# Pinned seven-product pairs with own raw buffers for the quarter chunk, and four gate pairs computed the same way

## The chip, the cores and the metric

The kernel runs on one core of one Trainium2 chip. The metric is the device time of one execution in microseconds. The engines are named as in the profile: PE is TensorE (matmuls), PEld its weight loads, DVE is VectorE, ACT is ScalarE, POOL is GpSimd, and SP is SyncE, which here issues DMAs only.

## The reference

One decoder layer on x of 512 tokens by 1024 channels, all in float32:

```python
proj = h @ w_in[l]
q, k, v, p, g = jnp.split(proj, ...)            # 512 each for q, k, v, p; 2048 gate logits
y_attn = moba_attention(q, k, v, rel_bias) @ w_branch_attn
y_pool = multiscale_pool(p, w_pool_group, pool_scale) @ w_branch_pool
gates = jax.nn.sigmoid(g).reshape(B, S, 2, D)
mixed = gates[:, :, 0] * y_attn + gates[:, :, 1] * y_pool
h = layer_norm(ALPHA * h + mixed @ w_out, ln1_g, ln1_b)
a, u = jnp.split(h @ w_ffn_in, 2, axis=-1)       # 2816 channels each
a = causal_dwconv(a, conv_w, conv_b)             # three taps
f = (jax.nn.gelu(a) * u) @ w_ffn_out
h = layer_norm(ALPHA * h + f, ln2_g, ln2_b)
```

Attention has 8 heads of 64 channels; the pool branch takes trailing means of 2, 4, 8 and 16 tokens.

## The kernel before

**Precision.** A float32 operand is split into a high part `hi` (a copy in the matmul's float32r type, on ACT, L69) and a low part `lo` (the rest, on DVE, L70). Each product of the mathematics is three matmuls, hi x hi, hi x lo and lo x hi (`mm3`, L183 to L186). Activations are kept transposed, channels on the partitions and 512 tokens along the free side.

**Weights.** The weights come as chunks of 128 x 1024 (512 KB), in one list `chunks` in order of use: v, the q/k/p/g tiles, the branch projections (`BR0`), the output projection (`WO0`), the FFN input (`FI0`) and the FFN output (`FO0`). `weights(i)` fetches up to `LEAD` = 3 chunks ahead of the one it returns, not past `state["limit"]`. `fetch` loads a chunk by SP into one of three raw buffers (tag `wraw`) and splits it into one of `RING` = 5 buffers each of `whi` and `wlo`.

**Stages.** v; then `in_tile` for the q, k, p and g tiles in the list `order`, 24 matmuls of 512 columns for a tile (8 blocks of the contraction, three matmuls each), with the g tiles as filler between the parts of the attention, pair of heads by pair of heads (`scores`, `trans`, `pv`; `bg` issues the next filler tile). There are 16 gate tiles, g0 to g15; tile f and tile 8 + f gate the same output channels of the two branches. The first twelve to be done are copied by DVE into `gates` (L355) and their sigmoid is taken later; the last four (`NLATE`) are written by ACT as sigmoids to `late`. After the attention, zT and oT (the outputs of the two branches before projection) are split, then the remaining gate tiles run, then the branch projection (`br`), the output projection (`wo`), layer norm, the FFN input (`fi`), the FFN output (`fo`), and the last layer norm.

**The seven-product pairs.** In the FFN input, f = 4 to 17 (`SEVEN`) take the pair of tiles (a, u), each 1024 x 128, as one block matrix with the tokens halved (t1, t2) and the contraction halved (k1, k2), and compute it with seven block products instead of eight, in Strassen's manner (`seven`, L693). The products use four combinations of the activations, nT1, T3, nT2 and T4 (`t_form`, L663, formed once), and four weight chunks for each f:

- A: the tile a, loaded by SP;
- X: u + a (with halves exchanged), loaded by SP as u (L131) and then added to by POOL with an accumulating DMA from a (L132); it goes to one of two buffers `xraw` (`fetch_sums`, called when X is within `AHEAD` = 5 chunks);
- D: half of u, 512 wide, loaded by SP into a `wraw` buffer;
- Y: formed by DVE from A and X in two halves (L144) in a `wraw` buffer.

A pair is seven groups (`s_mm`) of twelve matmuls of 256 columns, 84 in all, where two plain tiles have 48 of 512. The groups go to three banks, `sa`, `sb` and `sc`, in the order A, X, (the close of the pair before), Y, A, D, X. The close is the seventh group, on Y; DVE and ACT combine the products in between: the close needs DVE's addition of `y` and `sc` into `sa` (L711). Then comes `gated` (convolution, GELU, product).

**What sets the order.** The kernel is written in program order, and the framework schedules it: it simulates the engines by its own cost model and gives each engine a fixed queue, which the engine then runs in order, waiting at each instruction for its operands and for its output buffer. Only instructions issued under `tc.keep_in_program_order` keep their order among themselves.

Of the kernel before, what the change touches and what calls it, by code (L numbers as in the profile page):

```python
# [45 lines left out]
def layer_kernel(ctx: ExitStack, tc: tile.TileContext, xT, x, w_v, w_c, rel_bias, invcnt, w_group,  # L46
# [18 lines left out]
    def split(hi, lo, src, copy=None):  # L65
        if copy:
            copy(hi, src)
        else:
            nc.scalar.activation(hi, src, AF.Copy)  # L69
        nc.vector.tensor_tensor(lo, src, hi.bitcast(F32), op=ALU.subtract)  # L70

# [10 lines left out]
    chunks += [w_c[first[n] + j] for n, j in order]  # L82
    BR0 = len(chunks)
# [3 lines left out]
    FI0 = len(chunks)  # L87
    fi_at = {}
    for f in range(NF):
        for q in "AXDY" if f in SEVEN else "au":  # L90
            fi_at[f, q] = len(chunks)
            chunks.append((f, q) if f in SEVEN else w_fi[2 * f + "au".index(q)])
    FO0 = len(chunks)
# [28 lines left out]
    raws = {}  # L122
    sums = list(SEVEN)
    xu = None

    def fetch_sums(f):
        x_ = raws[f, "X"] = xu.tile([P, D], F32, tag="xraw", name=f"xraw{f}", bufs=2)
        a, u = w_fi[2 * f], w_fi[2 * f + 1]
        v = x_.rearrange("p (a c) -> p a c", a=2)
        (pst, pn), (est, _) = u.ap  # L130
        nc.sync.dma_start(v, bass.AP(tensor=u.tensor, offset=u.offset, ap=[[pst, pn], [0, 2], [est, S]]))  # L131
        nc.gpsimd.dma_start(v, bass.AP(tensor=a.tensor, offset=a.offset,  # L132
                                       ap=[[pst, pn], [u.offset + S - a.offset, 2], [est, S]]), accum_op=ALU.add)

    def fetch_seven(i, f, q):
        n = S if q == "D" else D
        if q == "X":
            raw = raws[f, "X"]
        else:
            raw = raws[f, q] = wp.tile([P, D], F32, tag="wraw", name=f"wraw{i}", bufs=3)[:, :n]  # L140
        if q == "Y":
            a, x_ = raws[f, "A"], raws[f, "X"]
            for c, o in ((slice(0, S), x_[:, S:]), (slice(S, D), raw[:, :S])):
                nc.vector.tensor_tensor(raw[:, c], o, a[:, c], op=ALU.add)  # L144
        elif q != "X":
            nc.sync.dma_start(raw, w_fi[2 * f] if q == "A" else w_fi[2 * f + 1][:, S:])
# [3 lines left out]
        return hi, lo  # L150

    def half(name, sl):
# [28 lines left out]

    def mm3(out_, w, a, start, stop, **kw):
        (wh, wl), (ah, al) = w, a  # L183
        nc.tensor.matmul(out_, wh, ah, start=start, stop=False, **kw)  # L184
        nc.tensor.matmul(out_, wh, al, start=False, stop=False, **kw)  # L185
        nc.tensor.matmul(out_, wl, ah, start=False, stop=stop, **kw)  # L186

# [153 lines left out]
    def in_tile(n):  # L341
        kind, j = order[n]
        wh, wl = split3(weights(C0 + n), KT)
        b = bank(f"{kind}{j}")
        for kt in range(KT):
            mm3(b, (wh[:, kt, :], wl[:, kt, :]), (xT_hi[:, kt, :], xT_lo[:, kt, :]), kt == 0, kt == KT - 1)
        if kind == "q":
            q_done(j, b)
        elif kind == "k":
            k_done(j, b)  # L350
        elif kind == "p":
            pool_in(j, b)
        elif len(gslot) < NKEEP:
            gslot[j] = gates[:, len(gslot), :]
            nc.vector.tensor_copy(gslot[j], b)  # L355
        else:
            gslot[j] = late[:, len(gslot) - NKEEP, :]
            nc.scalar.activation(gslot[j], b, AF.Sigmoid)

# [65 lines left out]
    def bg(n=1):  # L425
        for _ in range(n):
            if len(todo) > NLATE:
                t = todo.pop(0)
# [3 lines left out]
                if order[t][0] == "p":  # L432
                    due.append((t, order[t][1]))

    bg(3)
    for p in range(pairs):
        scores(2 * p)
        bg()
        scores(2 * p + 1)
        bg()  # L440
        trans(2 * p)
        bg()
        trans(2 * p + 1)
        bg()
        pv(p)
    bg(len(todo))
    attn.close()

    bra = ExitStack()
    bp = bra.enter_context(tc.tile_pool(name="bp", bufs=1, reuse_waits="tile"))  # L450
    late = bp.tile([P, NLATE, S], F32, name="late")
    zT_hi = bp.tile([P, 4, S], F32R, name="zT_hi")
# [5 lines left out]
    for k in range(4):  # L458
        split(oT_hi[:, k, :], oT_lo[:, k, :], oT[:, k, :])
    while todo:  # L460
        in_tile(todo.pop(0))
    mx_hi = act.tile([P, KT, S], F32R, tag="actT_hi", name="mx_hi")
    mx_lo = act.tile([P, KT, S], F32R, tag="actT_lo", name="mx_lo")
    ext = actp.enter_context(tc.tile_pool(name="ext", bufs=1, side="right"))
    for f in range(KT):
# [3 lines left out]
        for g in range(2):  # L469
            if gslot[8 * g + f].tensor is gates.tensor:  # L470
                nc.scalar.activation(gslot[8 * g + f], gslot[8 * g + f], AF.Sigmoid)
# [144 lines left out]
    def fi_mm(j, b, t):  # L616
        wh, wl = split3(weights(fi_at[j // 2, "au"[j % 2]]), KT)
        for kt in range(KT):
            mm3(b[:, t], (wh[:, kt, :], wl[:, kt, :]), (hT_hi[:, kt, t], hT_lo[:, kt, t]), kt == 0, kt == KT - 1)

# [29 lines left out]
    cuts = [slice(k, min(k + 4, KH)) for k in range(0, KH, 4)]  # L650
    t1, t2 = slice(0, 256), slice(256, 512)
    k1, k2 = slice(0, 4), slice(4, 8)

# [8 lines left out]

    def t_form(n):  # L663
        b11, b12, b21, b22 = (hraw[:, k, t] for k in (k1, k2) for t in (t1, t2))
        if n in ("nT1", "T3"):
            v, a = {"nT1": (b11, b11), "T3": (b12, b22)}[n]
            nc.vector.tensor_tensor(v, a, b12, op=ALU.subtract)
        else:
            v, a = {"nT2": (b22, b11), "T4": (b21, b22)}[n]
            nc.vector.scalar_tensor_tensor(v, a, -1.0, v, op0=ALU.mult, op1=ALU.subtract)  # L670
        split(*tt[n], v)

    for j in range(RING):
# [5 lines left out]
    for n in ("nT1", "T3", "nT2", "T4"):  # L679
        t_form(n)  # L680
    state["limit"] = len(chunks) - 1
    pending = []

    def s_mm(f, q, part, act_, b, start, skip=True):
        wh, wl = split3(weights(fi_at[f, q]), 4 if q == "D" else KT)
        for k in range(4):
            mm3(b, (wh[:, 4 * part + k, :], wl[:, 4 * part + k, :]), (act_[0][:, k, :], act_[1][:, k, :]),
                start and k == 0, k == 3, skip_group_check=not start)

    def whole(k, t):  # L690
        return hT_hi[:, k, t], hT_lo[:, k, t]

    def seven(f):  # L693
        ba, bb, bc = (bank(f"s{q}{f}") for q in "abc")
        chain, low, c11 = ba[:, 256:], bb[:, :256], bc[:, :256]
        y = ytiles[f % 2]
        u = xu.tile([P, S], F32, tag="u", name=f"u{f}", bufs=2)
        s_mm(f, "A", 0, whole(k1, t1), chain, True)
        nc.scalar.activation(y[:, t1], chain, AF.Copy)
        s_mm(f, "X", 0, tt["T3"], low, True)  # L700
        nc.scalar.activation(u[:, t2], low, AF.Copy)
        if pending:
            pending.pop()()
        s_mm(f, "Y", 0, tt["nT2"], chain, False)
        nc.scalar.activation(u[:, t1], chain, AF.Copy)
        s_mm(f, "A", 1, whole(k2, t1), c11, True)
        s_mm(f, "D", 0, tt["T4"], low, False)
        nc.vector.tensor_tensor(u[:, t1], u[:, t1], low, op=ALU.add)
        s_mm(f, "X", 1, tt["nT1"], chain, False)
        nc.vector.tensor_tensor(u[:, t2], u[:, t2], chain, op=ALU.add)  # L710
        nc.vector.tensor_tensor(ba[:, t1], y[:, t1], c11, op=ALU.add)  # L711

        def close():
            s_mm(f, "Y", 1, whole(k2, t2), chain, False)
            gated(f, ba, u, -1.0)

        pending.append(close)

    hr.close()
    xus = ExitStack()  # L720
    xu = xus.enter_context(tc.tile_pool(name="xu", bufs=1, reuse_waits="tile"))
    last = max(SEVEN)
    for f in range(RING // 2, last + 1):
        if f in SEVEN:
            seven(f)
            continue
        for j in range(max(RING, 2 * f), 2 * f + 2):
            hb[j] = bank(f"fi{j}")
            fi_mm(j, hb[j], slice(0, S))
            if pending:  # L730
                pending.pop()()
        gated(f, hb[2 * f], hb[2 * f + 1])

    spread = []
    for f in range(last + 1, NF):
        for j in range(2 * f, 2 * f + 2):
            hb[j] = bank(f"fi{j}")
            fi_mm(j, hb[j], slice(0, S))
            if pending:
                pending.pop()()  # L740
                xus.close()
# [191 lines left out]
```

## Time and profile before

| | |
|---|---|
| median of 3 runs | 651.3 us (651.03 to 653.6) |
| the profiled execution | 649.74 us, its span 648.0 us |
| granted TensorE clock, mean | 0.996 |
| busy PE, PEld | 635.7 us (98%), 551.4 us (85%) |
| busy DVE, ACT, POOL | 449.5 us (69%), 328.0 us (51%), 111.6 us (17%) |
| DMA | 94.79 MB, mean 146 GB/s |

In a row of the profile's timeline stand the start in us from the span's beginning, the duration, engine, line, operation, and the tiles written and read (numbers left out of names). `SPq` is a DMA issue on SP's queue. A bracket at the end tells how long the engine had stood idle and what ended it. In the windows, the columns after the stretch are its length, then busy us and instructions of PE, PEld, DVE, ACT and POOL, the granted TensorE clock, the DMA share and GB/s. A row of the waits reads: engine and tile that waited, the tile waited for, us in total, times, the longest. The rows of DMA issues give the number, the KB of each and the median us from issue to landing.

### The profile page before, as it was taken

The numbers are of one execution on the slowest core, as the hardware profiler recorded it, in microseconds if no ns is written. First come the engines' busy times: TensorE is split into PE (matmuls) and PEld (weight loads), VectorE is DVE, ScalarE is ACT, GpSimd is POOL, SyncE is SP. The second block draws the span as 40 slices with busy tenths as digits, with TensorE's granted clock in tenths as the row PEclk, the third lists the DMA queues.
The fourth block names the chain that finished last, engine by engine and source line by source line (L and its number), as shares of the span: only waits on it lengthen the run. The fifth ranks groups of instructions, "written<-read, shape, count | busy, mean of one in ns | idle before, by whom it ended". The sixth has DMA issues, their size and how long they took to land.

```text
span 648.0 us, 9322 instructions
## 1 busy us (share of the span) xinstructions
PE 635.7 (98%) x3586; PEld 551.4 (85%) x3586; DVE 449.5 (69%) x666; ACT 328.0 (51%) x475; POOL 111.6 (17%) x153
## 2 busy tenths in 40 slices
PE   9999999999999999999999999999999999999994
PEld 6888787877888888888999999998998888888884
DVE  6466665564532576299667888787986859698596
ACT  6547556675522333215444556455665337465452
POOL 1605361211000123300010101010100201123302
PEclk9999999999999999999999999999999999999998
DMA  9643222212222227404056686677635895989905
GB/s 323 197 166 99 82 81 82 74 67 89 74 95 98 91 98 286 136 1 162 2 150 173 170 208 155 179 179 188 165 128 163 274 264 137 218 188 193 282 4 129
DMA packets 32540, 94.79 MB, mean 146 GB/s; under 512 B 3688, under 2 KB 3944, under 8 KB 32240
## 3 DMA queue, kind: packets, MB, share of 16 engines
q1 hardware_dynamic: 22832, 66.91, 30.4%
q0 software_dynamic: 9088, 26.24, 20.7%
q10 hardware_dynamic: 576, 1.05, 0.5%
q8 instruction: 28, 0.46, 0.3%
q14 instruction: 16, 0.13, 0.1%
HBM read 91.02 MB, written 3.17 MB: 145 GB/s over the span
## 4 chain that ended last, share of the span: by engine, by line
PE 91%; DVE 3%; POOL 2%; DMA 1%; ACT 1%; issue 1%; DVEq 0%; ACTq 0%; POOLq 0%
PE fi L186 5%; PE fi L184 5%; PE fi L185 5%; PE g L184 5%; PE g L186 4%; PE g L185 4%; PE sa L184 4%; PE sa L186 4%; PE sa L185 4%; PE v L285 3%; PE wo L186 2%; PE br L186 2%; PE br L184 2%; PE wo L184 2%; PE wo L185 2%; PE br L185 2%
## 5 line engine op out<-in xcount | busy, mean ns | idle before, releaser
L70 DVE TENSOR_TENSOR wlo<-wraw,whi 128x1024 fp32r<-128x1024 f32 (+1 forms) x119 | 144.1, 1214 | 59.2 <-ACT whi L69 57.7
L69 ACT ACTIVATE whi<-wraw 128x1024 fp32r<-128x1024 f32 (+1 forms) x118 | 117.2, 996 | 131.9 <-PE g L185 23.6
L186 PE MATMUL fi<-hT_hi,wlo 128*128 128x512 f32 (+1 forms) x168 | 56.7, 339 | 0.0
L185 PE MATMUL fi<-hT_lo,whi 128*128 128x512 f32 (+1 forms) x168 | 56.7, 339 | 0.0
L184 PE MATMUL fi<-hT_hi,whi 128*128 128x512 f32 (+1 forms) x168 | 56.4, 340 | 0.0
L184 PE MATMUL g<-xT_hi,whi 128*128 128x512 f32 x128 | 50.3, 393 | 0.0
L186 PE MATMUL g<-xT_hi,wlo 128*128 128x512 f32 x128 | 49.9, 390 | 0.0
L185 PE MATMUL g<-xT_lo,whi 128*128 128x512 f32 x128 | 49.8, 389 | 0.0
L132 POOL DMA_DIRECT2D xraw<-in_w_fi x14 | 17.0, 1215 | 183.7 <-DVE y L624 70.2
L69 ACT ACTIVATE whi<-tw 128x1024 fp32r<-128x1024 f32 (+1 forms) x30 | 29.4, 982 | 21.6 <-DMA tw<-in_w_fo 8.1
L70 DVE TENSOR_TENSOR wlo<-tw,whi 128x1024 fp32r<-128x1024 f32 (+1 forms) x30 | 33.3, 1127 | 8.4 <-ACT whi L69 8.4
L185 PEld LDWEIGHTS fi<-hT_lo,whi 128*128 128x128 f32 x168 | 31.9, 190 | 3.5
L186 PEld LDWEIGHTS fi<-hT_hi,wlo 128*128 128x128 f32 x168 | 31.9, 190 | 3.3
L184 PEld LDWEIGHTS fi<-hT_hi,whi 128*128 128x128 f32 x168 | 31.6, 190 | 3.3
L184 PE MATMUL sa<-hT_hi,whi 128*128 128x256 f32 x112 | 31.9, 285 | 2.0 <-ACT whi L69 1.9
L186 PE MATMUL sa<-hT_hi,wlo 128*128 128x256 f32 x112 | 31.7, 284 | 0.0
L185 PE MATMUL sa<-hT_lo,whi 128*128 128x256 f32 x112 | 31.6, 283 | 0.0
L184 PE MATMUL sb<-T_hi,whi 128*128 128x256 f32 x112 | 31.5, 282 | 0.0
L184 PE MATMUL sa<-nT_hi,whi 128*128 128x256 f32 x112 | 31.5, 281 | 0.0
L186 PE MATMUL sa<-nT_hi,wlo 128*128 128x256 f32 x112 | 31.3, 279 | 0.0
L185 PE MATMUL sa<-nT_lo,whi 128*128 128x256 f32 x112 | 31.3, 279 | 0.0
L185 PE MATMUL sb<-T_lo,whi 128*128 128x256 f32 x112 | 31.3, 279 | 0.0
(250 smaller groups left out, 1762.8 us busy)
## 6 DMA issues: line engine op xcount, KB each, us to landing
wraw<-in_w_fi SPq DMA_DIRECT2D x30, 512.0 KB, 3.6
wraw<-in_w_c SPq DMA_DIRECT2D x28, 512.0 KB, 3.4
tw<-in_w_fo POOLq DMA_DIRECT2D x20, 512.0 KB, 8.3
xraw<-in_w_fi SPq DMA_DIRECT2D x14, 512.0 KB, 4.9
xraw<-in_w_fi POOLq DMA_DIRECT2D x14, 512.0 KB, 5.7
wraw<-in_w_fo SPq DMA_DIRECT2D x10, 512.0 KB, 5.1
tw<-in_w_fo SPq DMA_DIRECT2D x10, 512.0 KB, 6.6
wraw<-in_w_br SPq DMA_DIRECT2D x8, 512.0 KB, 3.3
```

Of the source, the lines that this page charges most:

```text
L69: nc.scalar.activation(hi, src, AF.Copy)
L70: nc.vector.tensor_tensor(lo, src, hi.bitcast(F32), op=ALU.subtract)
L132: nc.gpsimd.dma_start(v, bass.AP(tensor=a.tensor, offset=a.offset, ap=[[pst, pn], [u.offset + S - a.offset, 2], [est, S]]), accum_op=ALU.add)
L184: nc.tensor.matmul(out_, wh, ah, start=start, stop=False, **kw)
L185: nc.tensor.matmul(out_, wh, al, start=False, stop=False, **kw)
L186: nc.tensor.matmul(out_, wl, ah, start=False, stop=stop, **kw)
L285: nc.tensor.matmul(bs[j], xs_[j][a], (wh, wl)[b], start=kt == 0 and n == 0, stop=False)
```

## The change

Four things are changed.

1. All matmuls of the seven-product pairs are issued with `tc.keep_in_program_order`, and so are the matmuls of plain tiles while a close is pending (`pin` in `mm3`).
2. The chunk D gets raw buffers of its own: `draw`, two of them, in place of one of the three `wraw`.
3. The gate tiles g4 to g7 and g12 to g15 become four seven-product pairs. The list `order` now ends g2, g10, g3, then s4 to s7, then g11. For them x^T is fetched again in four quarters (`quad`, 512 KB each) and nT1, T3, nT2 and T4 of it are formed and split. The buffers (T-forms, two of `xrawg`, two of `drawg`, the quarters) lie in a pool `gx` in the space that the attention leaves. The sum X of a gate pair is fetched as in the FFN. `gates_done` takes both sigmoids on ACT straight from the result. All after T3's split is issued behind it (`issue_after`).
4. `late` moves to the other side of the memory, zT's and oT's splits come after the gate tiles, no gate pair's chunk is fetched until the attention is over (`state["limit"]`), and one filler tile at the last pair of heads is dropped.

`seven`, `s_mm`, `t_form` and the closing (`flush`) become general over the two uses. The core of the diff:

```diff
-    order += spare
+    order += [("g", 2), ("g", 10), ("g", 3)] + [("s", f) for f in range(4, KT)] + [("g", 11)]
...
+    for n, j in order:
+        at[n, j] = len(chunks)
+        if n == "s":
+            pair_of["g", j] = w_c[first["g"] + j], w_c[first["g"] + KT + j]
+            for q in "AXDY":
+                at["g", j, q] = len(chunks)
+                chunks.append((("g", j), q))
...
-        while sums and xu and fi_at[sums[0], "X"] <= i + AHEAD:
+        while sums and sums[0][0] in xpool and at[(*sums[0], "X")] <= i + AHEAD:
             fetch_sums(sums.pop(0))
...
-            raw = raws[f, "X"]
-        else:
-            raw = raws[f, q] = wp.tile([P, D], F32, tag="wraw", name=f"wraw{i}", bufs=3)[:, :n]
+            raw = raws[key, "X"]
+        elif q == "D":
+            raw = dpool[key[0]](key[1])
+        else:
+            raw = raws[key, q] = wp.tile([P, D], F32, tag="wraw", name=f"wraw{i}", bufs=3)
...
+    def t_form(n, tt, b11, b12, b21, b22):
...
+        if n != "nT1":
+            split_of[n] = split(*tt[n], v)
+        if n == "T4":
+            split(*tt["nT1"], b11)
...
+                start and k == 0, k == 3, tc.keep_in_program_order, skip_group_check=not start)
...
+        pin(nc.tensor.matmul(out_, wh, ah, start=start, stop=False, **kw))
+        pin(nc.tensor.matmul(out_, wh, al, start=False, stop=False, **kw))
+        pin(nc.tensor.matmul(out_, wl, ah, start=False, stop=stop, **kw))
...
+        if kind == "s":
+            seven(("g", j), (xT_hi, xT_lo), tg, p1s[j % 2], gus[j % 2],
+                  lambda ba, u, j=j: gates_done(j, ba, u))
+            return
...
+    def gates_done(j, ba, u):
+        nc.scalar.activation(new_gate(j), ba, AF.Sigmoid)
+        nc.scalar.activation(new_gate(KT + j), u, AF.Sigmoid, scale=-1.0)
...
+    gd = [gx.tile([P, S], F32, name=f"drawg{c}") for c in range(2)]
+    gr = [gx.tile([P, D], F32, name=f"xrawg{c}") for c in range(2)]
...
+            nc.sync.dma_start(v, xT[k.start * P:k.stop * P, t].rearrange("(k p) t -> p k t", p=P))
...
+    for n in ("nT1", "T3", "nT2", "T4"):
+        t_form(n, tg, *quads)
+    with ExitStack() as behind:
+        for ins in split_of["T3"]:
+            behind.enter_context(tc.issue_after(ins.ins))
+        while todo:
+            in_tile(todo.pop(0))
+        flush()
...
+    dpool["f"] = lambda f: xu.tile([P, S], F32, tag="draw", name=f"draw{f}", bufs=2)
+    xpool["f"] = lambda f: xu.tile([P, D], F32, tag="xraw", name=f"xraw{f}", bufs=2)
```

More of the change, by code (lines that the diff above doesn't have):

```diff
@@ L81, in layer_kernel @@
     C0 = len(chunks)
-    chunks += [w_c[first[n] + j] for n, j in order]
+    at = {}
+    pair_of = {}
+    for n, j in order:
[6 more added lines that the diff above has]
+        else:
+            chunks.append(w_c[first[n] + j])
     BR0 = len(chunks)
@@ L122, in layer_kernel, with fetch_sums @@
     raws = {}
[L123 to L128, printed above, removed]
+    sums = list(pair_of)
+    xpool = {}
+    dpool = {}
+    def fetch_sums(key):
+        x_ = raws[key, "X"] = xpool[key[0]](key[1])
+        a, u = pair_of[key]
         v = x_.rearrange("p (a c) -> p a c", a=2)
@@ L145, in fetch_seven @@
         elif q != "X":
-            nc.sync.dma_start(raw, w_fi[2 * f] if q == "A" else w_fi[2 * f + 1][:, S:])
+            a, u = pair_of[key]
+            nc.sync.dma_start(raw, a if q == "A" else u[:, S:])
         hi = wp.tile([P, D], F32R, tag="whi", name=f"whi{i}", bufs=RING)[:, :n]
@@ L426, in bg @@
         for _ in range(n):
-            if len(todo) > NLATE:
+            if order[todo[0]][0] != "s":
                 t = todo.pop(0)
@@ L469, in layer_kernel @@
         for g in range(2):
-            if gslot[8 * g + f].tensor is gates.tensor:
+            if 8 * g + f in plain:
                 nc.scalar.activation(gslot[8 * g + f], gslot[8 * g + f], AF.Sigmoid)
@@ L679, in layer_kernel @@
     for n in ("nT1", "T3", "nT2", "T4"):
-        t_form(n)
+        t_form(n, tt, *(hraw[:, k, t] for k in (k1, k2) for t in (t1, t2)))
     state["limit"] = len(chunks) - 1
[L682 to L717, printed above, removed]
     hr.close()
@@ L724, in layer_kernel @@
         if f in SEVEN:
-            seven(f)
+            seven(("f", f), (hT_hi, hT_lo), tt, ytiles[f % 2][:, t1],
+                  xu.tile([P, S], F32, tag="u", name=f"u{f}", bufs=2),
+                  lambda ba, u, f=f: gated(f, ba, u, -1.0))
             continue
```

125 lines of the change are left out of this document (87 added, 38 removed).

## The prediction

> **What bounds the kernel now.** I read the page first: which engine is full, and what ended the last wait on it.
>
> ```profile
> PE 635.7 (98%) x3586; PEld 551.4 (85%) x3586; DVE 449.5 (69%) x666; ACT 328.0 (51%) x475; POOL 111.6 (17%) x153
> PE   9999999999999999999999999999999999999994
> PE 91%; DVE 3%; POOL 2%; DMA 1%; ACT 1%; issue 1%; DVEq 0%; ACTq 0%; POOLq 0%
> xraw<-in_w_fi SPq DMA_DIRECT2D x14, 512.0 KB, 4.9
> xraw<-in_w_fi POOLq DMA_DIRECT2D x14, 512.0 KB, 5.7
> ```
>
> TensorE is busy in every slice and makes 91% of the chain that ended last, so fewer matmul columns shorten the kernel, as long as TensorE stays fed. The last two rows are the two transfers, one after the other, that make the chunk X = u + a of a pair; they decide my forecast. Next the stages that the change touches, by windows and by the timeline of PE:
>
> ```profile
> 180.00:212.00 32.00, 32.00 (x143) 26.50 (x142) 9.27 (x9) 9.01 (x12) 0.00 (x0) 1.00 0.29 99
> 367.00:389.00 22.00, 22.00 (x188) 22.00 (x187) 18.27 (x26) 12.42 (x19) 2.41 (x2) 1.00 0.73 191
> 399.00:412.00 13.00, 12.15 (x101) 11.80 (x100) 11.16 (x16) 8.10 (x12) 2.41 (x2) 1.00 0.60 169
> 434.00:445.00 11.00, 9.81 (x79) 9.38 (x79) 8.30 (x13) 5.18 (x7) 1.20 (x1) 1.00 0.74 174
> ```
>
> ```profile
> 179.87 0.39 PE L185 MATMUL g<-xT_lo,whi 128*128 128x512 f32 x1
> 180.09 0.39 PE L186 MATMUL g<-xT_hi,wlo 128*128 128x512 f32 x1
> ...
> 212.28 0.39 PE L184 MATMUL br<-zT_hi,whi 128*128 128x512 f32 x1
> ...
> 347.95 0.28 PE L184 MATMUL sa<-hT_hi,whi 128*128 128x256 f32 x1
> ...
> 410.84 0.28 PE L186 MATMUL sb<-T_hi,wlo 128*128 128x256 f32 x1
> 411.97 0.39 PE L184 MATMUL sa<-hT_hi,whi 128*128 128x256 f32 x1 [0.85 <-ACT whi L69]
> ...
> 441.98 0.28 PE L186 MATMUL sc<-hT_hi,wlo 128*128 128x256 f32 x1
> 443.34 0.39 PE L184 MATMUL sa<-hT_hi,whi 128*128 128x256 f32 x1 [1.08 <-ACT whi L69]
> ```
>
> The first window, gate tiles, is one unbroken row of 512-column matmuls, 32.00 / 143 = 0.224, by single starts 0.22 to 0.23 us; a tile of 24 takes 5.44. Gates end where br starts, 212.28. The seven-product stage begins at 347.95. Its 256-column matmuls are 0.117 us apart (22.00 / 188), TensorE's weight loading is then as full as TensorE, and a pair of 84 takes 9.97 at 0.1187, the mean over the stage. The last two windows are its only real holes: 411.97 - 410.84 and 443.34 - 441.98, less a pitch of 0.12 each, make 2.25, and the first matmul behind each takes 0.39 in place of 0.28: 2.5 us together.
>
> **The change part by part.** *Gate pairs.* Eight tiles of 24 (43.5 us) become four pairs of 84 (4 x 9.97 = 39.9): -3.7 if fed. *Pinning and own buffers for the quarter D.* Both holes are ACT splits of an A chunk that came late because its raw buffer, shared with D, came free late. With own buffers they go: -2.5. So the intent is worth -6.2.
>
> *What feeds TensorE.* Here the engines' orders decide, and each engine takes its queue in order. The present order around one X chunk, on DVE, SP and POOL:
>
> ```profile
> 403.58 0.68 DVE L144 TENSOR_TENSOR wraw<-xraw,wraw 128x512 f32<-128x512 f32 x1
> 404.19 1.22 DVE L70 TENSOR_TENSOR wlo<-xraw,whi 128x1024 fp32r<-128x1024 f32 x1
> 405.32 0.68 DVE L70 TENSOR_TENSOR wlo<-wraw,whi 128x512 fp32r<-128x512 f32 x1
> ...
> 406.52 0.74 DVE L624 SCALAR_TENSOR_TENSOR y<-sa,cvp,y 128x511 f32<-128x511 f32 x1
> ...
> 405.43 0.38 SPq L131 DMA_DIRECT2D xraw<-in_w_fi  x1
> ...
> 410.09 1.20 POOL L132 DMA_DIRECT2D xraw<-in_w_fi  x1 [8.22 <-DMA xraw<-in_w_fi]
> ```
>
> At 403.58 DVE forms the first half of Y(f), the sum of xraw(f) and A(f), and at 404.19 the low part of X(f) from the same xraw(f). That ends at 405.41; the buffer is free, and 0.02 us later SP loads u of pair f+2 into it; 4.66 us after that POOL adds a. So X(f+2) has two pairs' time, some 20 us, to come in, and the waits agree: by the row quoted below, DVE waited for an xraw transfer once in the whole run, at the start of the stage.
>
> In the changed program's order I find DVE forming Y(f+1) *ahead* of the low part of X(f), for f = 5 to 16. Y(f+1) needs xraw(f+1) complete; xraw(f+1) has the buffer of xraw(f-1) and is loaded only when DVE has done the low part of X(f-1). So a loop closes with one turn per pair: low part of X(f-1), SP's load, POOL's accumulation, Y(f+1) in two halves with a convolution step between, low part of X(f). Its turn, from the rows above and these (the landings of SP's loads, then of POOL's accumulations, the waits of DVE for xraw, and the low part of X(4)):
>
> ```profile
> DMA to landing us min/median/max: 3.6/4.9/6.5
> DMA to landing us min/median/max: 5.4/5.7/7.2
> ...
> 341.61 1.23 DVE L70 TENSOR_TENSOR wlo<-xraw,whi 128x1024 fp32r<-128x1024 f32 x1 [0.40 <-ACT whi L69]
> ...
> DVE wraw L144 <- DMA xraw<-in_w_fi: 4.9, 1, 4.9
> ```
>
> Load until POOL's issue: 5.2 (the median 4.9 with POOL's reaction; the row pair above gave 4.66). Accumulation 5.7. DVE 0.61 + 0.67 + 0.61 + 1.22 = 3.1 (start to start, the last to its end), handovers 0.1. Turn: 14.1 us, where TensorE needs a pair each 9.97. TensorE's third matmul on X(f) reads the low part, so it stands about 4 us per pair. The low part of X(4) ends at 342.8 (341.61 + 1.23) in the present timeline, whose stages before are the same work. Twelve turns lead to X(16): 342.8 + 12 x 14.1 = 512.0. Fed, TensorE would be there at 347.95 + 12 x 9.97 + 1.42 (the twelve matmuls of A) + 0.24 = 469.2. Late by 42.8; the closing group of pair 15 then waits for a DVE addition queued behind that low part, the splits of D and Y (0.7 and 1.2) and two other additions of some 0.4: 2.9 us, of which the rest of X's group covers 1, so about 2 more. X(17) is no longer in the loop, its buffer came free a turn earlier. Less the 2.5 of holes: +42.3. Bounds: at the shortest landings the turn is 3.6 + 5.4 + 3.2 = 12.2, +19.5; at 5.5 and 6.5 it is 15.2, +55.5; at both maxima 16.9, +76. I take the medians, as the same transfers run beside each other here (DMA share 0.60 to 0.74 in the windows).
>
> *Start of the gate pairs.* Around the end of attention:
>
> ```profile
> 141.95 0.40 PE L376 MATMUL sc<-kl,q 128*128 128x512 f32 x1
> ...
> 155.55 0.39 PE L185 MATMUL g<-xT_lo,whi 128*128 128x512 f32 x1
> ...
> 160.88 0.65 PE L417 MATMUL ob<-PT,vv 128*64 128x512 f32 x2
> ...
> 163.31 0.60 ACT L419 ACTIVATE oT<-ob 128x512 f32<-128x512 f32 x1 [0.96 <-PE ob L417]
> ...
> L667 DVE TENSOR_TENSOR hraw<-hraw x2: 1226/1226/1226, 316.1 to 317.4; 128x1024 f32<-128x1024 f32 x2
> ...
> 160.99 0.69 DVE L355 COPY gates<-g 128x512 f32<-128x512 f32 x1 [3.53 <-PE g L186]
> ```
>
> Both orders are the same up to 155.48. Then the changed TensorE queue has 17 matmuls of g3 (3.9 us) ahead of the end of the last ob (2.3 us): ob ends at 161.65. ACT copies oT, and the split of nT1 is queued behind that copy: 162.2 to 163.25. DVE waits for it and then has, in order: nT1's low part, T3, nT2, T3's low part (1.14 each start to start), the copy of g3 (0.61), T4, nT2's low part (1.14 each), half of Y(4) (0.61), and only then the low part of X(4) (1.22): 163.27 + 6 x 1.14 + 0.61 + 0.61 + 1.22 = 172.6. TensorE, with its remaining g3 and the group of A, would be at that operand at about 164.9: 7.7 us late. The loads hide: four fetches of x^T wait for the last score matmul and can go from 142.4 (141.95 + 0.40), and X(4) and X(5) behind them; their price without that cover would be one landing more, 5 us. The same loop then holds X(5) and X(6) (Y(6) stands ahead of X(5), Y(7) ahead of X(6)), without the convolution step: turn 13.4. X(6) has its low part at 172.6 + 2 x 13.4 = 199.4. Then the late close (+2.9), twelve groups of 1.424, g11 (5.44) and the last close (1.42): br starts at 226.3, that is +14.0 against 212.28, the -3.7 included. Bounds: turns of 11.5 give +10.2, of 14.5 give +16.2.
>
> The splits of zT and oT move behind the gates; four of each on ACT, by g11 and the close (6.9 us) covered, and uncovered they would cost some 4.5. The dropped filler tile and the direct sigmoids change where work lies and no amount: 0 (uncovered, a 0.6 ACT operation each).
>
> **Sum:** +42.3 + 14.0 = +56.3 on the profiled 649.74 is 706.0. The median of 651.3 is 1.6 above that execution: 707 against the median.
>
> [...] The accumulation took 5.4 at the least and 5.7 in the median. [...]
>
> **The rivals.** (1) *The sums are in time* and the plan holds: -6.2, 645. It needs a turn of at most 9.97, so both transfers in 6.8 us, where the shortest ones seen make 9.0; and the T-forms ready before 165, against ACT's order. For it: the present kernel streams the same bytes without a hole. It decides for faster as soon as the turn is under 9.97. Chance 0.06. (2) *The loop hides, the gate start does not*: +7.7 - 3.7 - 2.5 = +1.5, 653; the same condition on the turn, but the DVE queue at 163 stays. 0.04. (3) *Shorter transfers*: once TensorE stands 4 us per pair, other transfers thin out, and the accumulation has the queues alone. [...] Against it: the shortest accumulation of 14. 0.05. (4) *Longer turns* than 15.2, since X's load now goes out together with D's and A's each time: 723 and more, 747 at both maxima. 0.07.
>
> **How the numbers follow.** The forecast, a turn of 12.2 to 15.2, holds 0.78: 681 to 723 by its bounds (19.5 + 10.2 and 55.5 + 16.2 on the median), with 707 at the medians of the landings. The range 672 to 723 takes in (3) and leaves out (1), (2) and (4), 0.17. About 0.5% is what a measurement of this kernel can tell from no change: (1) is faster, 0.06; (2) within, 0.04; the rest slower, 0.90.
>
> **What would show it.** In the changed profile: in the seven-product stage X's low parts come some 14 us apart, TensorE's mean busy share there falls to about 0.7, its waits name wlo on DVE at the third matmul of sb, and next the addition sa on DVE; DVE's waits name the xraw transfers at the first half of Y, a dozen times. SP's X load starts right after a low part of X. Gates: the first sb of a gate pair waits till about 172, br starts near 226. I am wrong if br starts before 212, if the stage's pairs are 10 us apart, or if the two transfers together fall under 7 us.

## The result and the profile after

| | before | after |
|---|---|---|
| median of 4 runs, us | 651.22 (651.03 to 653.6) | 712.71 (711.69 to 713.98) |
| ratio, 95% interval | | 1.0936 [1.0903, 1.0969] |
| profiled execution: time, span | 649.74, 648.0 | 711.91, 710.2 |
| granted TensorE clock, mean | 0.996 | 0.962 |
| gates: last 128x512 copy of P^T on DVE to the first `br` matmul | 57.0 | 73.6 (+16.6) |
| FFN input: first matmul of a pair to the first `foe` matmul | 186.5 | 232.0 (+45.4) |

The kernel became slower by 9.4%. The two stages that the change touches hold all of it: 16.6 + 45.4 = 62.0, the spans differ by 62.2. From the page of after, the rows that answer to those of before, with the granted clock in 40 slices:

```profile
PE 656.8 (92%) x3730; PEld 574.7 (81%) x3730; DVE 468.3 (66%) x697; ACT 343.1 (48%) x499; POOL 114.2 (16%) x157
...
PE   8999999995889999999997987788779999999995
...
PEclk9999999998899999999999898889899999999999
...
xraw<-in_w_fi SPq DMA_DIRECT2D x14, 512.0 KB, 4.2
xraw<-in_w_fi POOLq DMA_DIRECT2D x14, 512.0 KB, 6.0
```

TensorE is full except in two places: slices 10 to 12, the start of the gate pairs, and slices 22 to 30, the seven-product pairs of the FFN. Its own busy time rose by 21 us, although the gate pairs have fewer columns: each matmul got longer where the clock fell (22.45 / 149 = 0.151 us of busy time at 0.82 in the second window below, 22.00 / 188 = 0.117 at 1.00 before). Windows of after (the columns as in the table of before):

```profile
364.71:398.00 33.29, 28.85 (x219) 28.45 (x218) 18.58 (x25) 14.18 (x23) 3.38 (x3) 0.90 0.57 138
454.00:482.00 28.00, 22.45 (x149) 21.63 (x149) 16.62 (x24) 11.40 (x17) 2.41 (x2) 0.82 0.53 132
528.20:542.00 13.80, 11.22 (x82) 11.02 (x81) 9.32 (x15) 5.50 (x10) 0.00 (x0) 0.88 0.24 77
```

Before, 22 us of this stage held 188 matmuls at a clock of 1.00; here 28 us hold 149 at 0.82. What TensorE and then DVE waited for, in the whole of after:

```profile
PE saf L253 <- DVE saf L213: 19.9, 11, 3.0
PE sbf L255 <- DVE wlo L70: 10.2, 5, 2.7
PE sbg L255 <- DVE wlo L70: 5.5, 3, 2.2
PE sbg L253 <- ACT whi L69: 5.4, 1, 5.4
```

```profile
DVE wraw L158 <- DMA xraw<-in_w_fi: 18.2, 5, 4.5
DVE wraw L158 <- issue: 14.5, 7, 2.7
```

DVE stood twelve times (5 + 7) at the first half of Y in the FFN, for 32.7 us; before, it stood there for an X transfer once. ("issue" is a wait for which the profile names no releaser. The turn below has one of these: the accumulation into its `xraw` landed at 398.55, and Y starts at 398.63.) TensorE's waits name the addition `saf` and the low part `wlo`, both of them DVE work queued behind that wait. The addition, on which the close waits, holds TensorE up for longer than the low part does (19.9 us against 10.2). One turn, by the timelines of DVE, SP, POOL and PE of after:

```profile
386.35 1.22 DVE L70 TENSOR_TENSOR wlo<-xraw,whi 128x1024 fp32r<-128x1024 f32 x1
387.59 0.38 SPq L143 DMA_DIRECT2D xraw<-in_w_fi  x1
392.42 1.21 POOL L144 DMA_DIRECT2D xraw<-in_w_fi  x1 [13.61 <-DMA xraw<-in_w_fi]
398.63 0.69 DVE L158 TENSOR_TENSOR wraw<-xraw,wraw 128x512 f32<-128x512 f32 x1 [1.94 <-issue]
399.24 0.74 DVE L738 SCALAR_TENSOR_TENSOR y<-saf,cvp,y 128x510 f32<-128x510 f32 x1
399.90 0.68 DVE L158 TENSOR_TENSOR wraw<-wraw,wraw 128x512 f32<-128x512 f32 x1
400.50 1.22 DVE L70 TENSOR_TENSOR wlo<-xraw,whi 128x1024 fp32r<-128x1024 f32 x1
...
387.62 0.38 PE L255 MATMUL sbf<-T_hi,wlo 128*128 128x256 f32 x1 [2.54 <-DVE wlo L70]
390.49 0.41 DVE L213 TENSOR_TENSOR saf<-y,scf 128x256 f32<-128x256 f32 x1
390.96 0.58 PE L253 MATMUL saf<-hT_hi,whi 128*128 128x256 f32 x1 [1.90 <-DVE saf L213]
```

The low part of X ends at 387.57, 0.02 later SP reloads the buffer, 4.83 later POOL adds, 6.21 later DVE can form Y, and 3.09 later the next low part has ended, at 401.72. Turn: 14.15. The chain of work that ended last can be followed back in after to about 519 us, and there it lies in the same loop (start, duration, piece):

```profile
519.47 3.85 DMA xraw<-in_w_fi
523.32 1.81 issue
525.13 0.69 DVE wraw L158
527.08 1.14 DVE wlo L70
```

At the gates:

```profile
163.04 0.60 ACT L503 ACTIVATE oT<-ob 128x512 f32<-128x512 f32 x1 [6.87 <-PE ob L501]
...
172.77 1.22 DVE L70 TENSOR_TENSOR wlo<-xrawg,whi 128x1024 fp32r<-128x1024 f32 x1
...
171.64 0.58 PE L253 MATMUL sbg<-gT_hi,whi 128*128 128x256 f32 x1 [5.39 <-ACT whi L69]
174.03 0.58 PE L255 MATMUL sbg<-gT_hi,wlo 128*128 128x256 f32 x1 [1.60 <-DVE wlo L70]
...
201.71 0.39 PE L255 MATMUL sbg<-gT_hi,wlo 128*128 128x256 f32 x1 [2.24 <-DVE wlo L70]
...
229.01 0.40 PE L253 MATMUL br<-zT_hi,whi 128*128 128x512 f32 x1
```

TensorE stood 7.0 us at the first X group of the gates, for ACT's split of X and then for DVE's low part of it, and 1.6 and 2.2 us at the X groups of the next two pairs.

### The profile page after: what moved, and what is told of

Read it like the earlier page. It is cut to its first block, busy times and chain, and to the rows that moved or that the text cites. A ratio compares the mean times of both kernels' runs of the same rounds, so it can differ in the third digit from the quotient of the medians.

```text
span 710.2 us, 9698 instructions
## 1 busy us (share of the span) xinstructions
PE 656.8 (92%) x3730; PEld 574.7 (81%) x3730; DVE 468.3 (66%) x697; ACT 343.1 (48%) x499; POOL 114.2 (16%) x157
## 5 line engine op out<-in xcount | busy, mean ns | idle before, releaser
L253 PE MATMUL saf<-hT_hi,whi 128*128 128x256 f32 x112 | 36.4, 325 | 19.9 <-DVE saf L213 19.9
L253 PEld LDWEIGHTS saf<-hT_hi,whi 128*128 128x128 f32 x112 | 24.4, 218 | 22.5 <-DVE saf L213 22.2
L255 PE MATMUL sbf<-T_hi,wlo 128*128 128x256 f32 x112 | 32.5, 290 | 10.3 <-DVE wlo L70 10.2
L255 PE MATMUL saf<-hT_hi,wlo 128*128 128x256 f32 x112 | 35.1, 313 | 0.0
L254 PE MATMUL saf<-hT_lo,whi 128*128 128x256 f32 x112 | 34.9, 311 | 0.0
L253 PE MATMUL saf<-nT_hi,whi 128*128 128x256 f32 x112 | 34.1, 304 | 0.0
L254 PE MATMUL saf<-nT_lo,whi 128*128 128x256 f32 x112 | 33.8, 301 | 0.0
L255 PE MATMUL saf<-nT_hi,wlo 128*128 128x256 f32 x112 | 33.6, 300 | 0.0
L253 PE MATMUL sbf<-T_hi,whi 128*128 128x256 f32 x112 | 31.8, 284 | 0.0
L254 PE MATMUL sbf<-T_lo,whi 128*128 128x256 f32 x112 | 31.6, 283 | 0.0
L158 DVE TENSOR_TENSOR wraw<-xraw,wraw 128x512 f32<-128x512 f32 x14 | 9.7, 692 | 33.1 <-DMA xraw<-in_w_fi 18.2
## 6 DMA issues: line engine op xcount, KB each, us to landing
wraw<-in_w_fi SPq DMA_DIRECT2D x30, 512.0 KB, 4.1
wraw<-in_w_c SPq DMA_DIRECT2D x24, 512.0 KB, 3.4
tw<-in_w_fo POOLq DMA_DIRECT2D x20, 512.0 KB, 8.2
xraw<-in_w_fi SPq DMA_DIRECT2D x14, 512.0 KB, 4.2
xraw<-in_w_fi POOLq DMA_DIRECT2D x14, 512.0 KB, 6.0
wraw<-in_w_fo SPq DMA_DIRECT2D x10, 512.0 KB, 5.8
tw<-in_w_fo SPq DMA_DIRECT2D x10, 512.0 KB, 6.7
wraw<-in_w_br SPq DMA_DIRECT2D x8, 512.0 KB, 3.6
```

What stands on the lines that cost most here:

```text
L253: pin(nc.tensor.matmul(out_, wh, ah, start=start, stop=False, **kw))
L254: pin(nc.tensor.matmul(out_, wh, al, start=False, stop=False, **kw))
L255: pin(nc.tensor.matmul(out_, wl, ah, start=False, stop=stop, **kw))
```

## The experiments

The theory to be tested: a scheduling order closes a loop (low part of X(f-1), reload, accumulation, Y(f+1), low part of X(f)), and the gate pairs start behind a long DVE queue. Against it stood: pinning TensorE costs time by itself; the transfers are slow by themselves; the lower clock, and not the wait, is the cause. All runs follow, each ratio against the kernel before as it ran beside them (its medians were 650.5 to 651.2). The two stages are measured as in the table above (change against before), in the profiled execution alone; the last copy of P^T stands at 155.3 to 157.5 us from one of them to the next, so the stages are compared and not the spans.

| run | median us | ratio [95%] | gates | FFN input | clock |
|---|---|---|---|---|---|
| after | 712.71 | 1.0936 [1.0903, 1.0969] | +16.6 | +45.4 | 0.962 |
| e5_pin_and_quarter | 694.1 | 1.0669 [1.0631, 1.0708] | 0.0 | +46.0 | 0.971 |
| e4_quarter_only | 665.16 | 1.0234 [1.0216, 1.0253] | 0.0 | +14.2 | 0.989 |
| e3_pin_only | 652.65 | 1.0036 [1.0023, 1.005] | 0.0 | +2.3 | 0.997 |
| e1_dve_order | 684.87 | 1.0537 [1.0509, 1.0565] | +13.1 | +22.3 | 0.984 |
| e10_no_accumulation | 681.22 | 1.047 [1.0451, 1.0488] | +19.1 | +13.0 | 0.975 |
| h3_order_fi | 651.6 | 1.0014 [1.0005, 1.0024] | 0.0 | +1.5 | 0.998 |
| h1_order_all | 662.19 | 1.0176 [1.0161, 1.0192] | +10.2 | +1.6 | 0.985 |
| h2_three_pairs | 657.36 | 1.0116 [1.0091, 1.0141] | +5.8 | +1.6 | 0.990 |
| l1_early_forms | 652.98 | 1.0029 [1.0017, 1.0042] | +1.2 | +1.6 | 0.997 |
| m4_fi_add_first | 647.6 | 0.9946 [0.9932, 0.996] | 0.0 | -3.1 | 0.998 |
| m2_all_in_order | 648.51 | 0.9956 [0.9941, 0.997] | +1.2 | -2.9 | 0.997 |

### The parts alone: pinning, own buffers, and both

These three go out from before and leave its plain gates. e3 pins the matmuls, e4 gives D its own buffers, e5 does both:

```diff
# e3, and in e5
-        nc.tensor.matmul(out_, wh, ah, start=start, stop=False, **kw)
+        pin(nc.tensor.matmul(out_, wh, ah, start=start, stop=False, **kw))
...
-                start and k == 0, k == 3, skip_group_check=not start)
+                start and k == 0, k == 3, tc.keep_in_program_order, skip_group_check=not start)
# e4, and in e5
+        elif q == "D":
+            raw = xu.tile([P, S], F32, tag="draw", name=f"draw{f}", bufs=2)
```

> The kernel before with the fixed order of the matmuls alone; D stays in the shared raw buffers and DVE has Y(f) ahead of the low part of X(f) as before. Theory: no loop, the holes at the A chunks stay: 651 us, 649 to 654. Rival A (the fixed order itself makes TensorE wait): 670 or more.

> The kernel before with own buffers for D alone. DVE's order then has Y(f+1) ahead of the low part of X(f) for f = 5, and half of it for f = 6 and 11, so two short stretches of the loop. Theory: two to three late turns of some 4 us, less the 2.5 us of holes at the A chunks: 655 us, 649 to 659. Rival C: 648.7, the holes gone.

> The kernel before with the fixed order of the matmuls and the own buffers for D, the gate tiles left plain. Theory: the FFN loop is there in full (Y(f+1) ahead of the low part of X(f) for f = 5 to 16) and the gates cost nothing: 651.2 + 45 = 696 us, 692 to 699. Rival C (the loss belongs to the gate pairs and what they shift): 649 to 655.

e5 has the whole FFN loss (+46.0 against +45.4) without gate pairs. Its waits of PE, and three of its low parts of X in a row:

```profile
PE sa L186 <- DVE sa L713: 21.1, 11, 3.1
PE sb L188 <- DVE wlo L70: 9.8, 6, 2.9
```

```profile
440.21 1.22 DVE L70 TENSOR_TENSOR wlo<-xraw,whi 128x1024 fp32r<-128x1024 f32 x1
...
454.00 1.22 DVE L70 TENSOR_TENSOR wlo<-xraw,whi 128x1024 fp32r<-128x1024 f32 x1
...
467.72 1.22 DVE L70 TENSOR_TENSOR wlo<-xraw,whi 128x1024 fp32r<-128x1024 f32 x1
```

They are 13.8 and 13.7 us apart. Neither part alone does the whole of it. Pinning alone keeps the order of Y and X of before and costs 0.36%. So the pinned TensorE order isn't what starves it.

e4 missed what I expected of it. Its DVE order has Y(f+1) whole ahead of X(f) at f = 5 only, and half ahead at 6 and 11. I had priced only the turn at those places. Its PE waits and two windows:

```profile
PE sa L186 <- DVE sa L713: 8.0, 5, 3.2
```

```profile
394.00:436.00 42.00, 40.51 (x337) 39.90 (x337) 33.90 (x48) 23.46 (x37) 4.82 (x4) 1.00 0.61 158
436.00:450.00 14.00, 10.79 (x71) 10.58 (x70) 8.83 (x13) 5.23 (x8) 1.20 (x1) 0.76 0.63 159
```

The close waited for the DVE addition behind the late Y, and around the longest of those waits (3.2 us) the clock was 0.76 over 14 us: 71 matmuls took 10.79 us of busy time, 0.152 each, where the window ahead has 40.51 / 337 = 0.120. Not all of e4 is accounted for by this: DVE's first halves of Y waited 18.2 us for X transfers in four places, and besides 11.7 us, in eight, for the A chunk. The second kind of wait was not in my sum, and no run tests what it costs.

### The order alone: Y behind the addition of the pair before

h1 is after, h3 is e5, each with one edge: the two additions that form Y(f+1) are issued behind the addition `saf<-y,scf` of pair f-1, so that the low part of X(f-1) and of X(f) stand ahead of them. No buffer, transfer or amount of work changes.

```diff
-            for c, o in ((slice(0, S), x_[:, S:]), (slice(S, D), raw[:, :S])):
-                nc.vector.tensor_tensor(raw[:, c], o, a[:, c], op=ALU.add)
+            with ExitStack() as behind:
+                if len(adds) > 1:
+                    behind.enter_context(tc.issue_after(adds[-2].ins))
+                for c, o in ((slice(0, S), x_[:, S:]), (slice(S, D), raw[:, :S])):
+                    nc.vector.tensor_tensor(raw[:, c], o, a[:, c], op=ALU.add)
...
-        nc.vector.tensor_tensor(ba[:, t1], y, c11, op=ALU.add)
+        adds.append(nc.vector.tensor_tensor(ba[:, t1], y, c11, op=ALU.add))
```

> Plain gate tiles, fixed order of the matmuls, own buffers for D, and one edge on DVE: both halves of Y(f+1) stand behind the addition sa<-y,sc of pair f-1. DVE's order is then low part of X(f), that addition, Y(f+1): the low part of X is neither behind the next Y nor ahead of its own, and X(f+1) has some 15 us to come in against the 11 us that its two transfers take. Theory as revised (a pair costs what the longest loop through DVE's order turns in, and only an order that leaves both ends slack gives TensorE's 10 us): the FFN's pairs come 10 us apart, its two holes of before are gone, 648.5 us, 647 to 652. Rival (with own buffers for D some other loop takes over, as it did in the run with X ahead of Y): 660 or more.

> The changed kernel with the same edge, gate pairs kept. Theory: the FFN as in the run with plain gates, and of the gate stage only its late start: 8 us of waiting for the low part of X(4), some 5 us by the slow clock behind it, less 3.7: br starts 8 to 13 us later than before, 660 us, 656 to 665. Rival (the loop in the gate stage is the larger part): br within 4 us of before, 652.

The order carries the loss: in the FFN 46.0 becomes 1.5 (h3) and 45.4 becomes 1.6 (h1), with the same transfers. The lower clock goes with the loop and isn't what came first: in after the window 364.71:389.78 stands at a clock of 1.00, and by its end the loop had turned twice, in 13.5 and 14.7 us, and TensorE had already waited 2.5 us. h1's gates still lose 10.2, now without the loop. PE's waits there, and two windows:

```profile
PE sbg L257 <- ACT whi L69: 5.4, 1, 5.4
...
PE sbg L259 <- DVE wlo L70: 1.6, 1, 1.6
...
PE sag L259 <- DVE wlo L70: 1.0, 1, 1.0
```

```profile
172.00:182.00 10.00, 7.41 (x32) 6.74 (x32) 7.77 (x10) 3.69 (x6) 1.19 (x1) 0.50 0.50 139
182.00:212.00 30.00, 30.00 (x252) 30.00 (x252) 17.97 (x25) 17.78 (x27) 1.20 (x1) 0.99 0.50 130
```

The waits make 8.0. Around and behind them TensorE ran at half clock: 32 matmuls at 7.41 / 32 = 0.232 where the next window has 30.00 / 252 = 0.119. The clock was 0.75 over 166 to 172, 0.50 over 172 to 182 and 0.97 over 182 to 192, which at half clock is some 169.0 to 182.6; TensorE was busy for 8.4 us of that, which makes 4.2 lost. Another 1.4 lies ahead of the pairs: before, the sixteen `ob` matmuls at the end of the attention go in one row, 2.30 us; with the changed order two of them stand alone ahead of g3's (1.07 us from the first's start to the second's end), and the sixteen take 3.30, the 48 matmuls of the plain gate tiles 11.29 in place of 10.93 (48 x 54.42 / 239). With the 3.7 that four pairs save, 8.0 + 4.2 + 1.4 - 3.7 = 9.9 of the 10.2. The 1.4 is in every run with gate pairs; which part of the change splits the `ob` row (the dropped filler tile is the likely one) wasn't tested.

h3 also shows that the 2.5 us of holes don't go by pinning and own buffers. They come back in another place. Its PE wait, and the DVE queue there:

```profile
PE sa L190 <- DVE sa L717: 2.2, 2, 1.1
```

```profile
398.34 1.22 DVE L763 TENSOR_TENSOR ra<-fT 128x1024 f32<-128x1024 f32 x1
399.48 1.22 DVE L70 TENSOR_TENSOR wlo<-wraw,whi 128x1024 fp32r<-128x1024 f32 x1
400.61 0.42 DVE L717 TENSOR_TENSOR sa<-y,sc 128x256 f32<-128x256 f32 x1
...
401.09 0.39 PE L190 MATMUL sa<-hT_hi,whi 128*128 128x256 f32 x1 [1.08 <-DVE sa L717]
```

A subtraction for the FFN output (`ra`) and the split of Y stand ahead of the addition that the close waits for. Two pairs wait so; most others come 10.19 us apart in place of 9.99, the step of m4 below.

### Another order: X ahead of Y, both pinned on DVE

e1 is after with the low part of X and the two halves of Y kept in program order on DVE, which gives X(f), then Y(f):

```diff
-                nc.vector.tensor_tensor(raw[:, c], o, a[:, c], op=ALU.add)
+                tc.keep_in_program_order(nc.vector.tensor_tensor(raw[:, c], o, a[:, c], op=ALU.add))
...
-        split(hi, lo, raw)
+        low = split(hi, lo, raw)[1]
+        if q == "X":
+            tc.keep_in_program_order(low)
```

> The changed kernel with one thing more: on DVE the low part of X and the two halves of Y keep the program's order, so Y(f+1) can no longer stand ahead of the low part of X(f). Theory (the loop of low part, load, accumulation and next Y turns in 14.1 us): both loops are gone, the FFN's pairs come 10 us apart, TensorE's clock there is back near 1.00, and only the late start of the gate pairs stays (8 us of waiting and the slow clock behind it, less 3.7): 656 us, 652 to 662. Rival A (it is the fixed order of the matmuls that makes TensorE wait): no change, 705 or more. Rival B (the throttle lowers the clock by itself, and the waits follow from it): clock near 0.96 again, 690 or more.

This missed. The loop through X's buffer is gone (TensorE no longer waits at `sbf`, the X group), but Y(f) is now formed only when X(f) is done, too late for its own group in `sa`:

```profile
PE saf L257 <- DVE wlo L70: 10.6, 14, 0.8
...
PE saf L255 <- ACT whi L69: 5.0, 7, 1.4
```

Pairs came 11.2 to 12.5 us apart. So "Y behind X" isn't the remedy. A place has to be found where Y is neither ahead of the low part that frees the buffer nor too late for its own group; h1 and h3 have it.

### The transfers alone: the turn without the accumulation

e10 is after, its queue order on DVE unchanged, but in the FFN X holds u alone: POOL's accumulation is left out.

```diff
-        nc.gpsimd.dma_start(v, bass.AP(tensor=a.tensor, offset=a.offset,
+        if key[0] == "g":
+            nc.gpsimd.dma_start(v, bass.AP(tensor=a.tensor, offset=a.offset,
```

> The changed kernel with POOL's accumulating transfer left out for the FFN's pairs, so X holds u alone there and the output is not the reference's; DVE's order is as in the changed kernel, with Y(f+1) ahead of the low part of X(f). Theory: the loop's turn falls by the 6 us of the accumulation to some 8 us, under TensorE's 10, so the order alone costs little: FFN pairs 10 to 10.5 us apart, 670 us, 666 to 676, all of the rest being the gate stage. Rival A (the fixed order of the matmuls or the clock): 700 or more.

The FFN's loss falls from 45.4 to 13.0: what the order costs is set by how long the transfers in the loop take. I had expected 670. Most pairs came 10.98 us apart (two 13.6) and not at TensorE's 9.97, and what is left is one wait:

```profile
PE saf L254 <- DVE saf L214: 10.1, 10, 1.9
```

DVE no longer waited for an X transfer; by its queue the addition stands behind the low part of X, which stands behind Y and a convolution step of the pair before, and that step needs the close, which needs the addition. This second, shorter loop is read from the queue and wasn't tested by itself. That run's gates, where nothing was changed, lost 19.1 in place of 16.6: TensorE's three waits at a low part of X made 6.0 us where they had made 5.5, the longest 4.0 in place of 2.2, and more of its time lay at a lower clock. The latter is an estimate: a mean of 0.975 over 680.6 us is worth 17.0 us, of which the FFN pairs have 3.2 (0.98 over 367 to 528) and some 2.6 are lost in before too (0.996 over 648.0), which leaves 11.2 for the gates, where after has 6.8 (0.50 over 171.32 to 181.56 and 202.04 to 205.46). So some us in this stage move with the program.

### The start of the gate pairs

h2 keeps h1's edge and makes only three gate pairs, with g4 and g12 as plain tiles between the end of attention and the pairs, as cover. l1 keeps four pairs and h1's edge and moves the chain itself: the four T-forms first on DVE, the splits of T3, nT2 and X(4) ahead of ACT's copy of oT, those of T4 and nT1 behind Y(4). Two smaller things go with it that the cut below leaves out: ACT's copy of a pair's first product stands behind the split of X, and two buffers lie elsewhere.

```diff
# h2
-    order += [("g", 2), ("g", 10), ("g", 3)] + [("s", f) for f in range(4, KT)] + [("g", 11)]
+    order += [("g", 2), ("g", 10), ("g", 3), ("g", 4), ("g", 12)] + [("s", f) for f in range(5, KT)] + [("g", 11)]
# l1, core
+        if tt is tg:
+            tc.keep_in_program_order(form)
+            if n == "T4":
+                with tc.issue_after(form.ins):
+                    for n, v in (("T3", b12), ("nT2", b22)):
+                        split_of[n] = split(*tt[n], v)
+            return
...
+    def rest():
+        with after_split((("g", 4), "Y")):
+            for n, k in (("T4", 2), ("nT1", 0)):
+                split(*tg[n], quads[k])
+            nc.scalar.activation(oT[:, pairs - 1, :], ob, AF.Copy)
```

> The same with three gate pairs (f = 5 to 7); tiles g4 and g12 stay plain and stand between the end of the attention and the first pair, 10.9 us of matmuls that cover the T-forms and the sums. Theory: TensorE does not stand at 163 to 174, the clock stays at 1.00, and the gate stage gains 3 x 0.9: br starts 2 to 3 us earlier than before, and with the FFN's holes gone 647 us, 645 to 651. Rival (the gate pairs themselves are fed too slowly by DVE, whatever the start): br later than before, 653 or more.

> Four gate pairs and the DVE edge as in the run with all pairs in order, and the start of the gate stage changed alone: the four T-forms come first on DVE, the splits of T3, nT2 and X(4) come ahead of ACT's copy of the last oT, the splits of T4 and nT1 behind Y(4), and drawg lies in space that is free before the attention's end. Theory (the late start is a queueing matter, ACT's copy behind ob and nine operations on DVE): the low part of X(4) ends near 167 instead of 174, TensorE stands 3 us at most, the clock stays near 1.00, br starts at 210 to 215 instead of 222.5, 651 us, 648 to 655. Rival (the sums or the fetched quarters of x^T are what is late): br at 219 or later, 659 or more.

h2 missed: 10.9 us of cover took only 4.4 from the loss, for the cover moved the chain along (the first low part of X ends at 178.2, in h1 at 174.0). DVE's queue in h2:

```profile
175.75 0.69 DVE L432 COPY gates<-g 128x512 f32<-128x512 f32 x1 [1.34 <-PE g L259]
...
176.96 1.22 DVE L70 TENSOR_TENSOR wlo<-xrawg,whi 128x1024 fp32r<-128x1024 f32 x1
```

The copy of the covering tile's result waits for TensorE to end that tile, and the low part of X stands two places behind the copy. In l1 the chain is short, its first low part ends at 167.7, and the gates lose 1.2 in place of 10.2:

```profile
PE sag L269 <- DVE wlo L70: 1.1, 2, 0.8
PE sbg L269 <- DVE wlo L70: 0.8, 1, 0.8
```

### All waits out of the FFN pairs

m4 is h3, and m2 is l1, with two more edges: the split of Y(f) behind the addition of pair f-1, and the subtraction `ra` behind the last pair's addition.

```diff
-        split(hi, lo, raw)
+        with tc.issue_after(adds[-1].ins) if q == "Y" and adds else ExitStack():
+            split(hi, lo, raw)
...
-            nc.vector.tensor_tensor(rd(c), side(0, c, t1), side(0, c, t2), op=ALU.subtract)
+            with tc.issue_after(adds[-1].ins):
+                nc.vector.tensor_tensor(rd(c), side(0, c, t1), side(0, c, t2), op=ALU.subtract)
```

> Plain gate tiles as in the first run with the DVE edge, and two edges more: the split of Y(f) stands behind the addition sa<-y,sc of pair f-1, and the two early subtractions ra<-fT stand behind the last pair. Theory: what was left in the FFN's pairs were waits of the close for that addition, twice 1.24 us with ra ahead of it and 0.2 a pair otherwise; with the addition 1.1 us earlier they go, pairs come 9.97 us apart, 648 us, 645.5 to 650. Rival (the shift of ra into the stage behind costs it back): 651 to 653.

> Both together: four gate pairs with the early start, and the edges of the run before in gates and FFN. Theory: the sum of the two, 651 - 3.5 = 647 us, 643 to 650, faster than the kernel before by 0.3 to 1%. Rival (the gate pairs stay short of operands): 652 or more.

m4, pinned pairs with own buffers for the quarter, three edges in DVE's order and plain gates, beats both kernels: 647.6, ratio 0.9946. In its pairs TensorE is busy without a gap:

```profile
348.00:487.00 139.00, 139.00 (x1162) 138.61 (x1161) 113.15 (x159) 81.16 (x123) 14.45 (x12) 1.00 0.68 167
```

So pinning and own buffers together with a fitting DVE order are worth 3.1 us in the FFN. How much of that is the order's alone isn't shown: the edges weren't run on the kernel before. m2 has nearly the same FFN (-2.9) and still +1.2 at the gates: the gate pairs brought no gain in any version. In l1 their 336 matmuls took 43.4 us, waits of 2.2 included, where the eight plain tiles need 43.7; the 1.4 ahead of them, of `ob` and the plain tiles, outweighs that.

## Why the prediction was right

It said 707, and 712.71 was measured; its mechanism is what the runs show. (Its own last sum, 706.0 + 1.6, makes 707.6 and so 708; nothing hangs on it.) FFN and gates were put at +42.3 and +14.0 and came to +45.4 and +16.6.

**The loop.** Right. One turn was put at 14.1; the low parts of X(5) and X(16) start at 371.61 and 526.99, 155.38 / 11 = 14.13. Up to X(16) the sum holds too: its third matmul came 123.5 us after the stage's start before (347.95 to 471.43) and 164.1 after (364.71 to 528.83), +40.6, where the forecast's 512.0 against 471.43 makes +40.6. The terms moved a little against each other: in the turn shown the load took 4.83 in place of 5.2, the accumulation 6.2 with its reaction in place of 5.7. Two signs came out otherwise. TensorE was to stand about 4 us per pair, first of all at the low part of X, at a busy share of 0.7; over the eleven turns it stood 27.6 of 155.4 us, a share of 0.82, and for longer at the close than at the low part. The rest of the lost time went into slower matmuls, at a mean clock of 0.89. The loop sets the pace either way. That the order is the cause is shown by h1 and h3 (order alone changed, loss gone), that the transfers set its size by e10, that the whole of it belongs to pinning and own buffers together, and not to the gate pairs, by e5 beside e3 and e4.

**The end of the FFN pairs** is the term that was mis-sized there. Behind X(16) I had about 2 us at one close, less a quarter of a us for the holes: +1.7. Measured: +45.4 - 40.6 = +4.8. The close waited 2.58, and the window 528.20:542.00 stands at a clock of 0.88, which over 13.8 us is 1.7: together 4.3 of the 4.8. The clock wasn't in my sum. Inside the loop no cost of it shows, for the turn stayed at 14.1: there it took the place of waiting.

**The start of the gates.** Right in mechanism: ACT's copy of oT, the split of nT1 behind it, DVE's queue, the low part of X(4). That ended at 173.99, forecast 172.6; the difference is there from the first link, oT at 163.04 against 161.7. The end of the last `ob` was counted too early: the 2.3 us for `ob` behind g3's matmuls is about right, but two more `ob` matmuls went ahead of g3, at 155.54, and took 1.0 by themselves. The term "0" for the dropped filler tile left this out as well. The low part of X(6) ended at 201.66 (forecast 199.4) and `br` began at 229.01 (226.3): of 2.7 missed, 1.4 lie in that link and 0.9 in the two turns.

**The intent, -6.2.** Two steps failed here, and they would have counted had the loop been absent. "With own buffers they go: -2.5" is wrong by itself: in h3, without the loop, the stage is 1.5 longer than before, because the close waits for the addition where it had waited for ACT (2.2 us in two waits), and most pairs come 0.2 us later. Only two more edges in DVE's order gave -3.1 (m4). And "-3.7 if fed" was never reached: with the best gate pairs (l1, m2) the stage is 1.2 us longer. Of the 4.9 between, in l1, 2.2 are waits, 1.4 lie ahead of the pairs in `ob` and the plain tiles, and 1.3 are a pitch of 0.123 between the waits where 0.1187 was reckoned.

**The rivals.** (1) and (2), the loop hidden, fell with the turn of 14.1. (2) also had its price too low: h1 is that case made on purpose, and its gates lose 10.2 where 7.7 - 3.7 = 4.0 stood; half clock (4.2) and the split `ob` row (1.4) were missing. (3), and with it 672 as the lower end of the range, rested on an accumulation time that no run shows. With TensorE standing and the DMA less busy (share 0.53 over 454 to 482, before 0.73 over 367 to 389), the 14 accumulations of after took 5.5 to 7.9, median 6.0; those of before had taken 5.4 to 7.2, median 5.7. (4) had longer turns, since X's load goes out with D's and A's; the loads got shorter (4.2 in the median, before 4.9).

## What to carry to other kernels

Where a scheduler fixes each engine's queue, look for an instruction that waits for a load and stands ahead of the one that frees the buffer for the next load: the loop then turns at the speed of its transfers, here 14.1 us where TensorE needed 10, although no engine is full. Price it by adding one turn from rows of the old trace, and repair it with an edge that puts the consumer behind the release and not later than its own use; both sides cost time here (+45.4 us in the FFN in after, +22.3 in e1). Fixing TensorE's order gained nothing here until the engines that feed it had a fitting order (e3 and h3 against m4).

## What the hardware showed that I had not expected

In these traces the granted clock was lower around or behind several waits of TensorE, and for some us past their end. In h1, with waits of 5.4, 1.6 and 1.0 that end at 171.62, 174.01 and 178.09, it was 0.75 over 166 to 172, 0.50 over 172 to 182 and 0.97 over 182 to 192. It was 0.76 over the 14 us around a wait of 3.2 (e4), 0.82 over 28 us with waits of 2.7, 0.9 and 1.9 (after, 454 to 482). Two single waits of 1.1 left no mark on it (h3, 0.998 over the whole span). So these holes cost more than their length: in h1 4.2 us on top of 8.0. In after nine stretches ahead of the kernel's end stand at 0.50: of 3.4 us (from 202.04, 475.11, 519.48 and 533.13), of 6.8 (from 389.78, 430.74, 458.04 and 502.42) and of 10.2 (from 171.32).

Shorter waits had it behind them too: one of 2.6 in after (to 532.74; 0.50 from 533.13 to 536.55) and one of 2.6 in e4 (to 387.10; 0.88 over 380 to 394). Of the waits of 1.9 in after, one had it (to 475.16; 0.50 from 475.11 to 478.52) and another had not (to 489.14; 1.00 over 478.52 to 502.42).
